# MLP up product by halves of the tokens, with all seven split weights of a block held

## The chip, the cores and the metric

The kernel runs on one core of one Trainium2 chip. The metric is the time of one execution on the device in microseconds (us). Before the change the median of 3 runs is 2862.23 us, the lowest 2861.79 and the highest 2864.47.

## The reference

One inference step of a trunk with two layers (DEPTH = 2), D_MODEL = 1024, D_FF = 4096. The prompt (16 meta tokens and 1024 frames) and 32 sample frames share the weights. Layer 0 mixes by a windowed attention and a gated linear attention, layer 1 by a forgetting attention; after each mixer comes the MLP, and only the MLP and the norm in front of it are touched here:

```python
def mlp(h, w_up, w_down):
    u = jax.nn.relu(h @ w_up)
    return (u * u) @ w_down
...
        xp = xp + mlp(rmsnorm(xp, norm_mlp[l]), w_up[l], w_down[l])
        xs = xs + mlp(rmsnorm(xs, norm_mlp[l]), w_up[l], w_down[l])
```

## The kernel before, in words

All arithmetic is fp32. TensorE multiplies in a reduced form (fp32r), so each operand is split into a high and a low part (hi_lo, L62): ScalarE casts the high part (L64), VectorE subtracts it from the source to give the low part (L66), or GpSimd does that where the caller passes "g" (L68). Each product of two operands is then three matmuls, hi by hi, hi by lo and lo by hi (mm3, L72 to L77).

The activations of a layer stay in SBUF as xT, features on the partitions, tokens on the columns. The tokens are four quarters q0 to q3 of 268 columns in layer 0 and 264 in layer 1 (qw); a half c has one column range of two quarters. The MLP's up product is done with seven products in place of eight for each 2x2 of blocks (list UP): the weights A11, A12, A22 and the sums S1 to S4 are multiplied by the activations B11, B21, B22 and the differences T1 to T4. A block is 128 columns of each half of w_up; there are 16 blocks, seven products in each, and each product has two token halves c = 0, 1 of 4 x 3 = 12 matmuls. That makes 16 x 7 x 2 x 12 = 2688 matmuls a layer. In the tables below a "group" is such a set of 12.

- **Operands.** After the mixer's output projection adds a quarter into xT (L833), mlp_norm squares it on ScalarE (L134), adds the squares on VectorE and GpSimd (L136), takes the mean on TensorE (L145), and scales the quarter on VectorE (L873, eight instructions). For q0 and q1 the result is split into B11 and B21; for q2 and q3 mlp_sums makes T1 (L884), T2 (L886), T3 (L888) and T4 (L890) on VectorE and splits each and B22. One such instruction has 128 x 1072 elements. All these subtractions and the low parts are VectorE's.
- **Weights.** up_load (L903) brings the raw block by a DMA from SyncE's queue, up_weights makes S1 to S4 (L914, L917, L920, L923) and splits each weight into a tile mu_w of five buffers, four products ahead of TensorE.
- **Order.** The loop in up takes a block product by product, and in each product both token halves. In mlp, TensorE's instructions stand in the order of the code (tc.manual_schedule); those of the other engines and of SyncE's queue are ordered by a scheduler that runs over the whole program. mlp makes T and B22 of q2 (first half), then squares q3 with two products of block 0 put between squares and scale, then makes T and B22 of q3 (second half).
- **Results.** Copies and adds from PSUM (ScalarE L974, L978, L980, L983; VectorE L976, L981, L985), squares (L989, L996) and the four differences that the down product needs (L1000) lie in columns of xT that are no longer needed; a DMA on SyncE's queue (L1001) writes them to ud in HBM, block by block. A separate tile, mu_early, takes part of block 0.
- **Down product.** down loads the weights k1 with four DMAs of 1 MB (L1018), splits all sixteen weight rows into md_w0 to md_w15, loads the activations ud as md_ur (L1058, three ahead), splits them into md_u, and runs 14 passes of 16 x 12 matmuls. Small GpSimd copies (behind, L1064) hold the loads of k2 back until a given md_u is there.

## Time and profile before

| | |
|---|---|
| median of 3 runs | 2862.23 us |
| profiled execution, its time | 2855.66 us |
| its span, mean granted TensorE clock | 2853.9 us, 0.963 |
| busy: PE, DVE, ACT, POOL | 92%, 66%, 44%, 20% |
| up product, layer 0 and layer 1 | about 619 to 973 us, 2137 to 2486 us |
| DMA traffic | 393.77 MB, 138 GB/s on average |

The profile is one execution, seen by the hardware profiler; its times count from the start of the span. PE is TensorE, DVE VectorE, ACT ScalarE, POOL GpSimd, SP SyncE (SPq its DMA queue). A row of the timeline gives the start, the busy time of a run of like instructions, the engine, the line, out<-in with the tiles' names, and their number; in brackets stands how long the engine had been idle and what ended that. Matmuls overlap by a little, so the start-to-start step of two rows is the better measure of one. A row of the table by stretches gives the busy time and the number of instructions (x) of PE, its weight loads (PEld), DVE, ACT and POOL, then the granted clock, the busy share of the DMA engines and GB/s.

### The profile page before, as it was taken

Reading aid. Unit: us, or ns where it says so; the run is one execution under the profiler, and the core shown is the slowest. Engines: PE = TensorE matmul, PEld = TensorE weight load, DVE = VectorE, ACT = ScalarE, POOL = GpSimd, SP = SyncE. Lnnn points to the kernel's source line nnn. Section 1 sums busy time; section 2 is a strip of 40 time slices with the busy share of each in tenths; the row PEclk is TensorE's granted clock in tenths of the full one; section 3 lists DMA queues with packets and bytes.
Section 4 is the critical chain, followed back from the end, with each engine's and each line's share of the span. In section 5 each row is a group of like instructions: output and inputs, shape, how many; then the busy total and the mean of one; then the engine's idle time right before and its main releaser. Section 6 shows DMA issues by size and latency. Waiting matters only on the chain.

```text
span 2853.9 us, 49119 instructions
## 1 busy us (share of the span) xinstructions
...
## 2 busy tenths in 40 slices
...
GB/s 192 100 134 104 72 140 45 30 120 101 151 129 164 202 231 218 168 134 121 123 193 168 115 176 127 89 101 102 77 91 79 144 147 144 164 274 205 200 138 105
DMA packets 371286, 393.77 MB, mean 138 GB/s; under 512 B 41503, under 2 KB 300280, under 8 KB 369000
## 3 DMA queue, kind: packets, MB, share of 16 engines
...
q8 instruction: 145, 2.38, 0.4%
q14 instruction: 93, 0.76, 0.1%
HBM read 263.94 MB, written 125.48 MB: 136 GB/s over the span
## 4 chain that ended last, share of the span: by engine, by line
PE 63%; issue 16%; DVE 9%; DMA 3%; ACT 2%; SPq 1%; POOL 1%; DVEq 0%; ACTq 0%; POOLq 0%
PE bank L75 11%; PE bank L76 11%; PE bank L77 11%; PE mu_y L77 5%; PE mu_y L76 5%; PE mu_y L75 5%; PE bank L1470 2%; PE bank L1480 1%; PE bank L1481 1%; PE fx_s L1452 1%; PE fx_s L1453 1%; DMA md_raw<-in_w_down 1%; PE bank L257 1%; DVE gl_Q L600 1%; PE b L701 1%
## 5 line engine op out<-in xcount | busy, mean ns | idle before, releaser
L75 PE MATMUL bank<-pj_wh,h 128*128 128x384 f32 (+3 forms) x832 | 298.0, 360 | 9.4 <-ACT pj_wh L64 7.0
L77 PE MATMUL bank<-pj_wh,h 128*128 128x384 f32 (+3 forms) x832 | 295.9, 357 | 6.0 <-DVE h L66 4.8
L76 PE MATMUL bank<-pj_wl,h 128*128 128x384 f32 (+3 forms) x832 | 297.3, 358 | 3.5 <-DVE pj_wl L66 3.5
L75 PE MATMUL mu_y<-md_u,md_w 128*128 128x268 f32 (+1 forms) x896 | 259.4, 289 | 26.9 <-ACT md_u L64 26.9
L76 PE MATMUL mu_y<-md_u,md_w 128*128 128x268 f32 (+1 forms) x896 | 257.8, 288 | 2.4 <-DVE md_u L66 2.4
L77 PE MATMUL mu_y<-md_u,md_w 128*128 128x268 f32 (+1 forms) x896 | 257.3, 287 | 0.0
L75 PE MATMUL bank<-md_u,md_w 128*128 128x268 f32 (+1 forms) x896 | 257.1, 287 | 0.0
L77 PE MATMUL bank<-md_u,md_w 128*128 128x268 f32 (+1 forms) x896 | 255.2, 285 | 0.0
L76 PE MATMUL bank<-md_u,md_w 128*128 128x268 f32 (+1 forms) x896 | 254.9, 285 | 0.0
L64 ACT CAST md_u<-md_ur 128x536 fp32r<-128x536 f32 (+1 forms) x224 | 141.1, 635 | 210.7 <-PE mu_y L77 110.7
L66 DVE TENSOR_TENSOR md_u<-md_ur,md_u 128x536 fp32r<-128x536 f32 (+1 forms) x224 | 157.9, 710 | 114.2 <-ACT md_u L64 113.8
L76 PE MATMUL mu_y<-ho_T,mu_w 128*128 128x268 f32 (+1 forms) x768 | 219.8, 286 | 0.2 <-DVE ho_T L66 0.2
L77 PE MATMUL mu_y<-ho_T,mu_w 128*128 128x268 f32 (+1 forms) x768 | 219.9, 286 | 0.0
L75 PE MATMUL mu_y<-ho_T,mu_w 128*128 128x268 f32 (+1 forms) x768 | 219.2, 285 | 0.0
L75 PEld LDWEIGHTS mu_y<-md_u,md_w 128*128 128x128 f32 x896 | 171.1, 191 | 27.4 <-ACT md_u L64 27.3
L66 DVE TENSOR_TENSOR mu_w<-mu_raw,mu_w 128x512 fp32r<-128x512 f32 x160 | 110.0, 688 | 117.0 <-ACT mu_w L64 117.0
L1283 POOL TENSOR_TENSOR fx_p<-fx_p,sm_den 128x144 f32<-128x144 f32 (+7 forms) x128 | 150.6, 1177 | 181.8 <-DVE sm_den L1282 164.7
L64 ACT CAST mu_w<-mu_raw 128x512 fp32r<-128x512 f32 x160 | 99.2, 622 | 188.6 <-PE bank L77 124.6
L75 PEld LDWEIGHTS bank<-pj_wh,h 128*128 128x128 f32 x832 | 158.8, 191 | 22.3 <-ACT pj_wh L64 7.5
L76 PEld LDWEIGHTS mu_y<-md_u,md_w 128*128 128x128 f32 x896 | 170.9, 191 | 3.5 <-DVE md_u L66 3.4
L77 PEld LDWEIGHTS bank<-pj_wh,h 128*128 128x128 f32 x832 | 158.6, 191 | 17.5 <-DVE h L66 5.1
L76 PEld LDWEIGHTS bank<-pj_wl,h 128*128 128x128 f32 x832 | 159.0, 191 | 16.3 <-DVE pj_wl L66 5.2
...
## 6 DMA issues: line engine op xcount, KB each, us to landing
...
ud<-xT SPq DMA_DIRECT2D x16, 1876.0 KB
...
```

Of the source, the lines that this page charges most:

```text
L64: nc.scalar.copy(hi, src)
L66: nc.vector.tensor_tensor(lo, src, hi.bitcast(F32), op=ALU.subtract)
L75: mm(out, ah, bh, start=start, stop=False)
L76: mm(out, ah, bl, start=False, stop=False)
L77: mm(out, al, bh, start=False, stop=stop)
L257: nc.tensor.matmul(*args, start=k == x == 0, stop=k == KB - 1 and x == 1)
L600: eng.tensor_tensor(ov, xv[r, :, :, 1], qv[r, :, :, 1], op=ALU.mult)
L701: nc.tensor.matmul(po[:m, h % 2, h // 2], att[:, h, :m], v[:, P * h:P * h + P], start=True, stop=False)
L1283: nc.gpsimd.tensor_tensor(p[:, :n], p[:, :n], den[:, 0:1].to_broadcast([P, n]), op=ALU.mult)
L1452: nc.tensor.matmul(s[:, a:b], qa[:, qc], ka[:, t0 + a:t0 + b], start=True, stop=False)
L1453: nc.tensor.matmul(s[:, a:b], qb[:, qc], kb[:, t0 + a:t0 + b], start=False, stop=ma >= mb)
L1470: nc.tensor.transpose(pt[:m, P * j:P * j + P], pr[j][:, k0:k0 + m], self.ident)
```

## The change

- **Order of the up product.** The unit is now one block and one token half. Block 0's first half goes first: A11, A12, S2, S1, S3. From then on the remaining products of a unit alternate with the first of the next one, by the list `late`. Every weight is used for half 0 and five or more groups later for half 1, so all seven split weights of a block are held, each in its own tile of one buffer; the next block's version is made after the half-1 use.
- **Who makes the low parts.** Block 0's seven weights, T4 and B22 have their low parts made on POOL (the "g" of hi_lo). The square of B21 goes from DVE to ACT.
- **Start in mlp.** The squares of q3 stand first, then block 0's load and its seven weights, then mlp_sums(2), four product steps, the scale of q3 (now mlp_scale, L883) and mlp_sums(3). The operands of each token half have tiles of their own.
- **Places of the results.** Even blocks put theirs in the columns of q0 and q1, odd ones in those of q2 and q3. The write to ud is issued by POOL instead of SP.
- **Down product.** The first k1 load and three activation loads stand ahead of the other three k1 loads; only six weight rows are written ahead of the passes, the other ten inside the first pass.
- **Norm buffers.** The squares use three buffers of nm_t in place of four, and the small part that fed from lx_t or nm_f uses nm_t.

The core of the diff:

```diff
@@ -130,7 +130,7 @@
...
-            sq = acc[e] if first else sb.tile([P, QMAX], F32, name="nm_t", bufs=4)[:, :w]
+            sq = acc[e] if first else sb.tile([P, QMAX], F32, name="nm_t", bufs=3)[:, :w]
...
@@ -211,18 +211,18 @@
...
         if few:
-            t0 = (sb.tile([P, D], F32, name="lx_t", bufs=3) if n == 0 else sb.tile([P, 384], F32, name="nm_f"))[:, :KB * few]
...
+            for k0 in range(0, KB, 4):
+                t0 = sb.tile([P, w], F32, name="nm_t", bufs=bufs)[:, :4 * few].rearrange("p (k f) -> p k f", f=few)
...
@@ -849,15 +849,17 @@
...
+    def operand(self, x, src, q, lo_eng="v"):
+        t = self.ho[x, q % 2]
+        self.hi_lo(src, t[:, 0], t[:, 1], lo_eng)
...
@@ -865,15 +867,20 @@
...
     def mlp_norm(self, q, between=()):
-        nc = self.nc
-        y = self.norm(self.qs[q], between)
+        finish = self.squares(self.qs[q])
+        for step in between:
+            step()
+        self.mlp_scale(q, finish())
...
+    def mlp_scale(self, q, y):
         c0, c1 = self.qs[q]
         x = self.xT[:, :, c0:c1]
         for k in range(KB):
...
+            self.nc.vector.scalar_tensor_tensor(x[:, k], x[:, k], self.gain[:, 2 * self.l + 1, k:k + 1], y, op0=ALU.mult, op1=ALU.mult)
...
@@ -885,121 +892,130 @@
...
-        sub(b21, b21, b11)
-        self.operand("T4", b21, q)
-        self.operand("B22", b22, q)
...
+        self.operand("T4", b21, q, "g")
+        self.operand("B22", b22, q, "g")
...
-    def up_load(self, b, sb):
...
+    def up_load(self, b, pool):
+        raw = pool.tile([P, KB, 2, P], F32, name=f"mu_raw{b % 2}", bufs=1)
...
+    def up_weights(self, x, w, pools, lo_eng):
...
             src = {"A11": a11, "A12": a12, "A22": a22}[x]
-        hl = sb.tile([P, 2, 4, P], F32R, name="mu_w", bufs=5)
-        self.hi_lo(src, hl[:, 0], hl[:, 1])
+        hl = pools[x not in ("A11", "A12")].tile([P, 2, 4, P], F32R, name=f"mu_w{x}", bufs=1)
...
-        early = sb.tile([P, hw], F32, name="mu_early", bufs=1)
+        units = [(b, c) for b in range(self.NP) for c in range(2)]
+        order = [(0, "A11"), (0, "A12"), (0, "S2"), (0, "S1"), (0, "S3")]
+        for u in range(len(units)):
+            late = [(u + 1, "A11"), (u, "A22"), (u + 1, "A12"), (u, "S4"), (u + 1, "S2"), (u + 1, "S1"), (u + 1, "S3")]
+            order += [x for x in late if x[0] < len(units)]
...
+        def weights(b, x):
+            ws[b, x] = self.up_weights(x, raws[b], pools, "v" if b else "g")
+
+        load(0)
+        for x in ("A11", "A12", "S1", "S2", "S3", "A22", "S4"):
+            weights(0, x)
+        yield
+        load(1)
+        for u, wn in order:
+            b, c = units[u]
+            w = ws[b, wn]
...
+            act = self.ho[self.UP[wn], c]
...
+            if wn == "A11":
+                if c == 0 and b:
+                    load(b + 1)
...
+            for k in range(4):
+                self.mm3(out, (w[:, 0, k], w[:, 1, k]), (act[:, 0, k], act[:, 1, k]), first and k == 0, k == 3, wn in ("S2", "S3", "A22", "S4"))
+            t = {x: y[:, cc] for x, y in v.items()}
+            if wn == "A11":
+                nc.scalar.copy(t["B11"], out)
...
+                nc.scalar.copy(t["B12"], out)
+            elif wn == "S3":
+                nc.scalar.copy(t["B22"], out)
+                tt(t["B22"], t["B22"], pr["z", u], op=ALU.add)
...
-                nc.sync.dma_start(self.ud[b // 4][:, b % 4], place[:, b % 2, 1:8, :hw])
...
+                        tt(v[x], v[p], v[m], op=ALU.subtract)
+                    nc.gpsimd.dma_start(self.ud[b // 4][:, b % 4], place[:, 1:8])
+
...
+                    for x in {"S2": (), "S1": ("S1", "S2")}.get(wn, (wn,)):
+                        weights(b + 1, x)
             yield
 
...
@@ -1063,8 +1079,6 @@
...
-        for x in range(4):
-            load(k1[x], "A11", 4 * x, 4)
...
@@ -1074,7 +1088,11 @@
...
-        for kb in range(NP):
+        load(k1[0], "A11", 0, 4)
+        ready(0)
+        for x in range(1, 4):
+            load(k1[x], "A11", 4 * x, 4)
+        for kb in range(6):
             w[0, kb] = weights(0, kb)
         at = 0
         out = {}
...
@@ -1088,6 +1106,8 @@
...
+                if n == 0 and c == 0 and kb + 6 < NP:
+                    w[0, kb + 6] = weights(0, kb + 6)
...
@@ -1132,14 +1152,19 @@
         with ExitStack() as st, tc.manual_schedule(engines={mybir.EngineType.PE}):
             ps = st.enter_context(tc.tile_pool(name="mlp", bufs=4, space=PSUM, reuse_waits="tile"))
             self.nm = pool(nms, "nml")
-            self.operands("ho2", ("T1", "T2", "T3", "T4", "B22"), "left")
-            with tc.tile_pool(name="mu", bufs=1, reuse_waits="tile") as sb:
-                steps = self.up(sb, ps)
-                self.mlp_sums(2)
-                self.mlp_norm(3, [partial(next, steps) for _ in range(2)])
-                self.mlp_sums(3)
-                for _ in steps:
-                    pass
+            pools = [pool(self.ups, "mua")]
+            self.operands("ho2", ("T2", "T1", "T3", "T4", "B22"), "left")
+            pools.append(pool(self.ups, "mub"))
+            finish = self.squares(self.qs[3])
+            steps = self.up(pools, ps)
+            next(steps)
+            self.mlp_sums(2)
+            for _ in range(4):
+                next(steps)
+            self.mlp_scale(3, finish())
+            self.mlp_sums(3)
+            for _ in steps:
+                pass
             self.ups.close()
             ks = ExitStack()
             kp = pool(ks, "mk", "right")

```

Line numbers after the change are larger by some: L884, L888, L886 and L890 (T1, T3, T2, T4) are L891, L896, L893 and L895, L914/L917/L920/L923 (S1, S2, S3, S4) are L921/L924/L926/L929, L873 is L883, L985 is L998, L989 is L1002, L1000 is L1013, L1001 is L1014, L1018 is L1034, L1058 is L1074. The lines L989 and L994 of after are the adds behind A12 and S3.

First place, the start of the up product in layer 0, VectorE. Before, around the scale of q3 (L873), the rows are the last weights of block 0, the sums of block 1, and the norm:

```order
L976 TENSOR_TENSOR mu_early<-mu_early,bank 128x268
L66 TENSOR_TENSOR mu_w<-mu_raw,mu_w 128x512
L976 TENSOR_TENSOR mu_early<-mu_early,bank 128x268
L66 TENSOR_TENSOR ho_T_6497<-xT,ho_T_6497 128x4x268
L66 TENSOR_TENSOR mu_w<-mu_raw,mu_w 128x512
L914 TENSOR_TENSOR mu_s<-mu_raw 128x512
L151 SCALAR_TENSOR_TENSOR nm_a<-bank,nm_a 128x268
L917 TENSOR_TENSOR mu_s<-mu_s,mu_raw 128x512
L920 TENSOR_TENSOR mu_raw<-mu_raw 128x4x128
L152 SCALAR_TENSOR_TENSOR nm_y<-nm_a,nm_y 128x268
L873 SCALAR_TENSOR_TENSOR xT<-xT,gain,nm_y 128x268 x8
L884 TENSOR_TENSOR xT<-xT 128x4x268
```

Ahead of the scale stand low parts of block 0's weights, the first sums of block 1 and the adds behind A12 of both halves; none of these rows reads a product later than A12. After, the rows around the scale of q3 (now L883) are:

```order
L929 TENSOR_TENSOR mu_raw_6542<-mu_raw_6542,mu_s 128x4x128
L66 TENSOR_TENSOR ho_T_6502<-xT,ho_T_6502 128x1072
L921 TENSOR_TENSOR mu_s<-mu_raw_6585 128x512
L989 TENSOR_TENSOR xT<-xT,bank 128x268
L926 TENSOR_TENSOR mu_raw_6585<-mu_raw_6585 128x4x128
L151 SCALAR_TENSOR_TENSOR nm_a<-bank,nm_a 128x268
L994 TENSOR_TENSOR xT<-xT,bank 128x268
L152 SCALAR_TENSOR_TENSOR nm_y<-nm_a,nm_y 128x268
L883 SCALAR_TENSOR_TENSOR xT<-xT,gain,nm_y 128x268 x8
L66 TENSOR_TENSOR mu_wA_6701<-mu_raw_6585,mu_wA_6701 128x512
L891 TENSOR_TENSOR xT<-xT 128x4x268
L66 TENSOR_TENSOR mu_wA_6732<-mu_raw_6585,mu_wA_6732 128x512
```

No low part of block 0's weights is left here. The scale now stands behind L994, which reads the result of S3, the fifth group of TensorE's new order; the second half's T1 to T4 (L891 and so on) come behind it.

The same place on POOL. Before, POOL has only the adds of squares and then nothing until the down product:

```order
L136 TENSOR_TENSOR nm_acc_6168<-nm_acc_6168,nm_t 128x268 x2
L136 TENSOR_TENSOR nm_acc_6325<-nm_acc_6325,nm_t 128x268 x2
L136 TENSOR_TENSOR nm_acc_6517<-nm_acc_6517,nm_t 128x268 x2
L1064 COPY md_k_10201<-md_u 1x1
L1064 COPY xT<-md_u 1x1 x4
```

After, these rows stand there (mu_wA and mu_wS are the seven weights of block 0, ho_B and ho_T are B22 and T4, first 6505 and 6506 for half 0, then 6510 and 6511 for half 1):

```order
L68 TENSOR_TENSOR mu_wA_6564<-mu_raw_6542,mu_wA_6564 128x512
L136 TENSOR_TENSOR nm_acc_6516<-nm_acc_6516,nm_t 128x268
L68 TENSOR_TENSOR ho_B_6506<-xT,ho_B_6506 128x1072
L68 TENSOR_TENSOR mu_wS_6553<-mu_s,mu_wS_6553 128x512
L68 TENSOR_TENSOR mu_wS_6561<-mu_raw_6542,mu_wS_6561 128x512
L68 TENSOR_TENSOR mu_wS_6557<-mu_s,mu_wS_6557 128x512
L68 TENSOR_TENSOR ho_T_6505<-xT,ho_T_6505 128x1072
L68 TENSOR_TENSOR mu_wS_6568<-mu_raw_6542,mu_wS_6568 128x512
L68 TENSOR_TENSOR ho_B_6511<-xT,ho_B_6511 128x1072
L68 TENSOR_TENSOR ho_T_6510<-xT,ho_T_6510 128x1072
L1014 DMA ud_6538<-xT 128x7x536 x4
L1014 DMA ud_6539<-xT 128x7x536 x4
```

POOL has taken five weight low parts (two more stand earlier), four low parts of 128 x 1072, and the ud writes.

Second place, the passage from the up to the down product of layer 0. VectorE before, where the rows md_w are the low parts of the down weights (the first twelve of the sixteen are left out) and md_u those of the activations:

```order
L66 TENSOR_TENSOR md_w_10248<-md_k_10200,md_w_10248 128x512
L66 TENSOR_TENSOR md_w_10251<-md_k_10200,md_w_10251 128x512
L66 TENSOR_TENSOR md_w_10254<-md_k_10200,md_w_10254 128x512
L66 TENSOR_TENSOR md_w_10257<-md_k_10200,md_w_10257 128x512
L66 TENSOR_TENSOR md_u<-md_ur,md_u 128x536 x3
L1032 TENSOR_TENSOR md_k_10201<-md_k_10201,md_raw 128x512 x3
```

and after:

```order
L1013 TENSOR_TENSOR xT<-xT 128x536 x4
L66 TENSOR_TENSOR md_w_10240<-md_k_10210,md_w_10240 128x512
L66 TENSOR_TENSOR md_w_10243<-md_k_10210,md_w_10243 128x512
L66 TENSOR_TENSOR md_w_10246<-md_k_10210,md_w_10246 128x512
L66 TENSOR_TENSOR md_w_10249<-md_k_10210,md_w_10249 128x512
L66 TENSOR_TENSOR md_u<-md_ur,md_u 128x536 x3
L66 TENSOR_TENSOR md_w_10252<-md_k_10211,md_w_10252 128x512
L66 TENSOR_TENSOR md_w_10255<-md_k_10211,md_w_10255 128x512
```

The three md_u rows that stood behind sixteen md_w rows stand behind four. The same place on SP's queue, before:

```order
L903 DMA mu_raw<-in_w_up 128x8x128 x2
L1001 DMA ud_6543<-xT 128x3752 x2
L1018 DMA md_k_10197<-in_w_down 128x4x512
L1018 DMA md_k_10198<-in_w_down 128x4x512
L1018 DMA md_k_10199<-in_w_down 128x4x512
L1018 DMA md_k_10200<-in_w_down 128x4x512
L1058 DMA md_ur<-ud_6540 128x2x268 x2
L1058 DMA md_ur<-ud_6541 128x2x268
L1018 DMA md_raw<-in_w_down 128x512 x2
L1001 DMA ud_6543<-xT 128x3752
L1018 DMA md_raw<-in_w_down 128x512
L1018 DMA md_k_10201<-in_w_down 128x4x512
```

and after:

```order
L910 DMA mu_raw_9288<-in_w_up 128x8x128 x2
L910 DMA mu_raw_9514<-in_w_up 128x8x128 x2
L910 DMA mu_raw_9740<-in_w_up 128x8x128 x2
L1034 DMA md_k_10210<-in_w_down 128x4x512
L1074 DMA md_ur<-ud_6538 128x2x268 x2
L1074 DMA md_ur<-ud_6539 128x2x268
L1034 DMA md_k_10211<-in_w_down 128x4x512
L1034 DMA md_k_10212<-in_w_down 128x4x512
L1034 DMA md_k_10213<-in_w_down 128x4x512
L1034 DMA md_raw<-in_w_down 128x512 x3
L1034 DMA md_k_10214<-in_w_down 128x4x512
L1074 DMA md_ur<-ud_6539 128x2x268
```

The ud writes have left the queue, so the loads of the down product stand directly behind the raw weights of the last block.

129 lines of the change are left out of this document (52 added, 77 removed).

## The prediction

> **What bounds the kernel now.** I read the page first: PE is busy for 92% of the span, so a change pays where PE is not busy. Then I cut the stretches around the two MLPs into windows; the columns are explained in the section on the profile.
>
> ```profile
> 600.00:620.00 20.00, 14.23 (x110) 13.60 (x108) 17.66 (x35) 9.66 (x19) 2.91 (x3) 1.00 0.39 116
> 620.00:640.00 20.00, 10.04 (x61) 9.62 (x60) 19.96 (x33) 8.02 (x14) 0.00 (x0) 0.76 0.52 144
> 640.00:660.00 20.00, 14.14 (x92) 13.61 (x93) 17.20 (x22) 9.58 (x15) 0.00 (x0) 0.73 0.04 10
> 680.00:960.00 280.00, 280.00 (x2273) 280.00 (x2272) 195.58 (x340) 94.64 (x202) 0.00 (x0) 1.00 0.44 138
> 960.00:980.00 20.00, 12.96 (x106) 12.74 (x104) 9.63 (x17) 6.43 (x14) 0.00 (x0) 0.87 0.59 221
> 980.00:1000.00 20.00, 12.92 (x82) 12.41 (x83) 13.44 (x23) 8.16 (x15) 2.75 (x7) 0.70 1.06 386
> 2140.00:2160.00 20.00, 9.88 (x60) 9.61 (x60) 19.96 (x33) 7.79 (x13) 0.00 (x0) 0.76 0.20 53
> 2180.00:2480.00 300.00, 300.00 (x2474) 300.00 (x2473) 205.94 (x362) 101.56 (x219) 0.00 (x0) 1.00 0.46 141
> ```
>
> In the middle of the up product PE is full: 2273 matmuls in 280 us, 0.1232 us each, 1.48 us per group of 12, at a clock of 1.00. VectorE (DVE) has 195.58 of 280 there, so it has room. At the start (620 to 640) it is the reverse: DVE 19.96 of 20, PE 61 matmuls where 162 fit, POOL nothing. At the passage to the down product (960 to 1000) both wait. Layer 1 repeats this. The waits of PE, from its timeline, are these:
>
> ```profile
> 619.58 0.39 PE L75 MATMUL mu_y<-ho_B,mu_w 128*128 128x268 f32 x1 [4.35 <-ACT mu_w L64]
> 622.21 0.59 PE L77 MATMUL mu_y<-ho_B,mu_w 128*128 128x268 f32 x1 [2.08 <-DVE mu_w L66]
> 643.73 0.59 PE L75 MATMUL bank<-ho_T,mu_w 128*128 128x268 f32 x1 [11.61 <-ACT ho_T L64]
> 646.23 0.59 PE L76 MATMUL bank<-ho_T,mu_w 128*128 128x268 f32 x1 [1.91 <-DVE ho_T L66]
> 986.29 0.59 PE L75 MATMUL mu_y<-md_u,md_w 128*128 128x268 f32 x1 [13.34 <-ACT md_u L64]
> 987.36 0.59 PE L76 MATMUL mu_y<-md_u,md_w 128*128 128x268 f32 x1 [0.47 <-DVE md_u L66]
> 2161.32 0.59 PE L75 MATMUL bank<-ho_T,mu_w 128*128 128x264 f32 x1 [10.52 <-ACT ho_T L64]
> 2499.10 0.59 PE L75 MATMUL mu_y<-md_u,md_w 128*128 128x264 f32 x1 [13.56 <-ACT md_u L64]
> ```
>
> So per layer there is a start of about 20 us of waiting, behind DVE's chain that makes the operands, and a passage of 13.8 us (13.34 + 0.47), behind DVE's low parts. The change acts on both.
>
> **The middle of the up product: no change.** The same 2688 matmuls run at PE's rate. DVE gains a little less work (the B21 square goes to ACT), ACT has 94.64 of 280. Each weight is now remade in a single buffer: between its half-1 use and its next use lie six other groups, 8.9 us. The tightest is S2, which needs S1 made first; it is worked out as a rival. I count zero.
>
> **The passage: a gain of about 7.5 us per layer.**
>
> ```profile
> 973.00 0.43 DVE L985 TENSOR_TENSOR xT<-xT,bank 128x268 f32<-128x268 f32 x1 [1.04 <-PE bank L77]
> 974.22 2.72 DVE L1000 TENSOR_TENSOR xT<-xT 128x536 f32<-128x536 f32 x4
> 976.85 9.82 DVE L66 TENSOR_TENSOR md_w<-md_k,md_w 128x512 fp32r<-128x512 f32 x16
> 986.59 1.96 DVE L66 TENSOR_TENSOR md_u<-md_ur,md_u 128x536 fp32r<-128x536 f32 x3
> ```
>
> Call 972.9, where the last group ends, E. DVE then finishes the results at 976.85 (E+3.9), makes sixteen low parts (9.82, 0.61 each) and only then the first md_u, so PE runs on from 987.36, E+14.5. After, the list has four low parts ahead of md_u: 3.9 + 4 x 0.61 + 0.65 = E+7.0, a gain of 7.5. The other twelve stand next on DVE at 0.61 each, faster than PE's 1.48 per weight row, so they stay ahead. PE still pauses for more than 3 us, so its slow clock after the pause (0.70 in the window) stays; it cancels. The k1 loads no longer queue behind ud writes; they land before E, which takes away ACT's waits there.
>
> What is late next: md_ur of the fourth group of activations. On SP it stands behind a k2 load that waits for a POOL copy, which itself stands behind POOL's last ud writes. Before, the load was issued at 987.85 and its DVE part ran at 998.12, 10.3 us later, with the queues at 1.06 and 386 GB/s:
>
> ```profile
> 987.85 0.53 SPq L1058 DMA_DIRECT2D md_ur<-ud  x1
> 998.12 0.71 DVE L66 TENSOR_TENSOR md_u<-md_ur,md_u 128x536 fp32r<-128x536 f32 x1
> ```
>
> After, it could issue at about E+8 and be ready at E+18; PE needs it six groups after E+7, with the slow clock for the first five us, at about E+18. So this may give back 0 to 3 us. I take 7.5, with 4 to 9 as bounds.
>
> **The start: a loss of about 6 us per layer.** Prices (start-to-start steps are 1.19 for 1072 elements, 0.60 for 512):
>
> ```profile
> 611.82 2.53 DVE L873 SCALAR_TENSOR_TENSOR xT<-xT,gain,nm_y 128x268 f32<-128x268 f32 x6
> 614.95 1.27 DVE L884 TENSOR_TENSOR xT<-xT 128x1072 f32<-128x1072 f32 x1
> 616.14 0.77 DVE L833 TENSOR_TENSOR xT<-xT,bank 128x268 f32<-128x268 f32 x2
> 621.47 0.68 DVE L66 TENSOR_TENSOR mu_w<-mu_raw,mu_w 128x512 fp32r<-128x512 f32 x1
> 622.07 0.68 DVE L914 TENSOR_TENSOR mu_s<-mu_raw 128x512 f32<-128x512 f32 x1
> 638.01 3.36 DVE L873 SCALAR_TENSOR_TENSOR xT<-xT,gain,nm_y 128x268 f32<-128x268 f32 x8
> ```
>
> Let t0 be 614.35, the end of q2's scale. Before, PE is free to go on with the second half's operand at 646.23, t0+31.9, with 61 up matmuls done. After, by PE's list, it stops before S2 of half 1, with nine groups, 108 matmuls, done. Those 47 more are worth 47 x 0.1232 = 5.8 us. When is the T2 of half 1 ready? DVE's list from t0 to T2 of half 0 has seven rows of 1072 elements, four of 512 and eight of 268 (0.35 each, by the 0.77 for two that overlap): 8.3 + 2.4 + 2.8 = t0+13.5. PE then runs S2 and S1, cold for five us (5.5), the mean (0.7) and S3 (1.5), t0+21.2; the add behind S3 and the end of the norm stand behind it, then the scale (3.4) to t0+26; then six rows of 1072, two of 512 and one add, 8.7, and 1.2 for T2's low part: t0+36. By this, 36 - 31.9 - 5.8 = -1.7, a small gain: the earlier products and the DVE work handed to POOL pay for a scale that now waits for S3.
>
> But POOL's part is not free. These rows show POOL and DVE at the same time:
>
> ```profile
> 1315.74 0.78 DVE L66 TENSOR_TENSOR h<-nm_t,h 128x268 fp32r<-128x268 f32 x2
> 1319.32 1.92 DVE L66 TENSOR_TENSOR h<-nm_t,h 128x268 fp32r<-128x268 f32 x2
> 1319.11 1.84 POOL L68 TENSOR_TENSOR h<-nm_t,h 128x268 fp32r<-128x268 f32 x2 [1.23 <-ACT h L64]
> 2120.52 3.06 POOL L136 TENSOR_TENSOR nm_acc<-nm_acc,nm_t 128x264 f32<-128x264 f32 x1 [4.69 <-ACT nm_t L134]
> 2120.57 2.41 DVE L66 TENSOR_TENSOR ho_B<-xT,ho_B 128x1056 fp32r<-128x1056 f32 x2
> 616.60 0.75 POOL L136 TENSOR_TENSOR nm_acc<-nm_acc,nm_t 128x268 f32<-128x268 f32 x1 [5.41 <-DVE xT L833]
> 1744.73 2.36 POOL L68 TENSOR_TENSOR fx_ml<-fx_ot,fx_mh 128x1024 fp32r<-128x1024 f32 x1 [1.62 <-ACT fx_mh L64]
> 1745.17 0.69 DVE L66 TENSOR_TENSOR fk_l<-bank,fk_h 128x512 fp32r<-128x512 f32 x1 [1.01 <-ACT fk_h L64]
> ```
>
> Two DVE low parts take 0.78 where they are not held up, but 1.92 behind POOL's two, and the four as a whole 2.13 (1319.11 to 1321.24), about the 1.5 (two at the 0.75 of 616.60, as wide) and 0.78 added up. At 2120.52 a POOL add of 0.75 takes 3.06: it ends half a microsecond after DVE's 2.41. So with both inputs in SBUF they take turns. Where DVE reads PSUM ("bank"), as at 1745.17 beside the POOL row of 1744.73, its 0.69 is that of 621.47.
>
> The Trainium skill ("SBUF — State Buffer", the section on the two separate sides) states this as a rule: a DVE operation with two SBUF inputs and a GpSimd operation that reads SBUF hold a shared port pair exclusively, and the loser blocks for the whole instruction. The trace agrees, 2.13 elapsed against 2.28 added; by the rule alone the start would cost the upper end below.
>
> POOL's rows at the start are five low parts of 512 at 1.25 (half of the 2.36 for 1024 elements, and some fixed time), two of 1072 at 2.45 and two adds at 0.75: 12.7 us, of which DVE's PSUM reads and waits cover some. I placed the rows of both lists one by one, each taking its turn when its operands are there and the other has ended, DVE first on a tie: T2 of half 0 is then at t0+19 and its weight at t0+21.5, and S2 of half 1 starts at t0+46. That gives 46 - 31.9 - 5.8 = +8.3; with POOL first, t0+48.4, +10.7. Between -1.7 and +10.7 the rows lie near +8.3; I take +6, since DVE's wait for S3 and its adds from PSUM may leave POOL more room than my turns do. The first wait of PE at t0 (4.35 + 2.08) goes in any case, since A11 now stands among the last projection groups, and is in the counts above.
>
> **Small terms.** Block 0's raw weights, 1 MB, now stand ahead of one load of the mixer's output weights on SP. At 386 GB/s that is 2.7 us if nothing covers it, else 0; I take 1 in layer 0, 0 in layer 1. The ud writes move to POOL:
>
> ```profile
> zb<-sw_z POOLq DMA_DIRECT2D x32, 194.0 KB, 2.3
> ud<-xT SPq DMA_DIRECT2D x16, 1876.0 KB
> ```
>
> POOL's own DMAs land 2.3 us after the issue for 194 KB. For 1876 KB that is 5 us at 386 GB/s, or 22 us scaled by size. The place is written again a block later, with some 12 us of slack, so I take 0. The Trainium skill ("DMA: Bandwidth & Descriptors", the anatomy of a GpSimd DMA) gives 2 us plus the bytes over 436 GB/s, an estimate of 6.4 us; by that the term is 0 as well, and no run here shows a large write on this queue.
>
> The norm buffers also shift the order of the first stage, where PE is idle for half of the first 50 us:
>
> ```profile
> 0.00:50.00 50.00, 23.56 (x119) 20.95 (x120) 20.43 (x56) 22.19 (x45) 10.80 (x13) 1.00 0.65 207
> ```
>
> Transposes of later chunks come earlier in the list, some projections later. The total work is the same; I take 0, within 5 either way.
>
> **Sum.** 2 x (+6 - 7.5) + 1 = -2 us on the profiled 2855.66. The median of the runs is 2862.23, 6.6 above it; the change is carried over to the median: 2860 us.
>
> **Rivals.**
> - *They don't take turns enough to matter.* The start gives -1.7 per layer: 2 x (-1.7 - 7.5) + 1 = -17, 2845 us. For it: 1744.73 and the DVE waits for PE, in which POOL is free. Against: 1319.11 and 2120.52.
> - *POOL goes first and the list is worse than worked out.* +10.7 per layer and 3 given back at the passage: 2 x (10.7 - 4.5) + 1 = +13, 2875 us. It decides where DVE finds POOL's two 1072 rows ahead of T1 and T2.
> - *The middle stalls, slower.* After the half-1 S1 group, DVE must make S1's low part, the S2 sum and S2's low part, behind the add of S3 and a square: 1.5 for S3, 0.8 for copy and add, then 0.6, 0.6, 0.7, 0.6, about 5 us, against five groups, 7.4 us. From 2.5 us more on (one run of four L1000 rows, 2.72, in between is enough) each block stalls. At 0.7 us in 30 blocks: +21, 2881 us. The same comes of ud writes that take over 12 us. Against: DVE idles for 30% of the middle.
> - *Not what it says:* the scheduler's list could have left DVE's chain as it was. The list shows otherwise, so this gets no share of its own.
>
> **Chances.** Forecast 0.48, turns without cost 0.25, POOL first 0.13, middle stalls 0.10, rest (first stage) 0.04. One measurement can tell about 0.2%, 5.7 us: faster than 2856.5, slower than 2868. The forecast's own range, 2853 to 2868, puts 0.11 of its 0.48 below 2856.5 and 0.02 above 2868. Faster: 0.25 + 0.11 = 0.36; slower: 0.13 + 0.10 + 0.02 + 0.02 = 0.27; same 0.37. For 8 in 10 the range takes in the first two rivals, 2842 to 2877, and leaves out the stalls and half of the edges.
>
> **What would show it.** Right: S2 of half 1 starts 40 to 46 us after the end of q2's scale, with POOL's L68 rows of 1072 elements over 3 us beside DVE's; PE's wait at the passage is about 6.5 in place of 13.34; windows in the middle stay 20.00 of 20. Wrong: PE waits inside the middle, a start before t0+38, or a passage above 10 us.

## The result, and the profile after

The changed kernel takes 2897.55 us (median of 4 runs, 2894.24 to 2900.16) against 2863.35 us before (4 runs, 2861.79 to 2867.05): a ratio of 1.0117, 95% interval 1.0099 to 1.0134. It is slower by 34 us, where 2860 us and a range up to 2877 us were forecast. The profiled execution took 2900.16 us, with a span of 2898.4 us and a mean TensorE clock of 0.950 (before 2855.66, 2853.9 and 0.963), so the two traces lie 44.5 us apart.

Cut at the same landmarks of PE, this is where the 44.5 us are (us; "up" runs from the last matmul of the output projection to the last one of the up product, "passage" from there to the first matmul of the down product's second pass, `bank<-md_u`; in layer 1 the projection's end is marked by its last matmul on the tile `fk_h`, some 4 us ahead of its very last one, before and after alike):

| stretch | before | after | difference |
|---|---|---|---|
| start to the second half of layer 0's output projection | 557.7 | 555.6 | -2.1 |
| second half of that projection | 57.2 | 63.9 | +6.7 |
| up, layer 0 | 357.8 | 368.8 | +11.0 |
| passage, layer 0 | 41.0 | 47.0 | +6.0 |
| down product to the first score product of layer 1 | 629.7 | 631.7 | +2.0 |
| layer 1 from there to the second half of its projection | 446.7 | 454.4 | +7.7 |
| second half of that projection | 36.7 | 37.0 | +0.3 |
| up, layer 1 | 358.4 | 370.8 | +12.3 |
| passage, layer 1 | 41.3 | 41.8 | +0.5 |
| down product to the end | 327.3 | 327.4 | +0.1 |

The places that the change touches (projections, up, passages) hold 36.8 us, about the 34 us of the medians. The 7.7 us in the middle can be chance for the greater part: that stretch took 446.7 to 451.3 us in four profiled kernels whose MLP start is that of before, and 447.9 to 457.3 us in the ten others of this study. A mean difference of some 3 us between the two groups is left unexplained.

The windows of the changed kernel, for the stretches shown of before (same columns):

```profile
620.00:640.00 20.00, 1.29 (x11) 1.08 (x9) 20.00 (x17) 8.16 (x13) 13.29 (x7) 0.59 0.16 55
660.00:680.00 20.00, 13.50 (x91) 13.51 (x92) 15.41 (x19) 8.40 (x14) 2.49 (x1) 0.71 0.00 1
680.00:960.00 280.00, 280.00 (x2268) 280.00 (x2268) 189.76 (x324) 101.09 (x215) 13.85 (x14) 1.00 0.43 144
980.00:1000.00 20.00, 11.02 (x75) 10.29 (x74) 10.01 (x17) 5.61 (x11) 2.91 (x6) 0.81 0.59 199
1000.00:1020.00 20.00, 11.25 (x72) 10.74 (x71) 13.02 (x22) 8.47 (x15) 1.50 (x2) 0.76 1.06 387
```

The middle of the up product is as full as before. The window 620 to 640 is the one to look at: DVE reads 20.00 of 20 busy, but with 17 rows where it had 33, and POOL is busy for 13.29 where it had nothing. Busy time counts the time in which an instruction is held up. The rows differ in size, so their number alone is no measure; but at the start-to-start steps of rows that nothing held up (1.19 us for 1072 elements, 0.60 for 512, 0.35 for 268) the 17 rows are an estimated 11.4 us of work, where the 33 of before were the full 20. Some 8.6 us DVE stood still. PE had 61 matmuls there and now has 11. From 660 to 680 PE is short once more, where before it was busy for 20.00 of 20. At the passage it is short over two windows, from 980 to 1020.

PE's waits in the changed kernel, from its timeline, first the two starts, then the two passages:

```profile
641.54 0.59 PE L75 MATMUL mu_y<-ho_T,mu_wS 128*128 128x268 f32 x1 [20.25 <-ACT xT L987]
666.50 0.59 PE L75 MATMUL mu_y<-ho_T,mu_wS 128*128 128x268 f32 x1 [11.13 <-ACT xT L987]
996.59 0.59 PE L75 MATMUL mu_y<-md_u,md_w 128*128 128x268 f32 x1 [8.05 <-ACT md_u L64]
997.64 0.59 PE L76 MATMUL mu_y<-md_u,md_w 128*128 128x268 f32 x1 [0.46 <-DVE md_u L66]
1015.88 0.59 PE L75 MATMUL mu_y<-md_u,md_w 128*128 128x268 f32 x1 [6.97 <-ACT md_u L64]
1018.25 0.59 PE L76 MATMUL mu_y<-md_u,md_w 128*128 128x268 f32 x1 [1.78 <-DVE md_u L66]
2188.92 0.59 PE L75 MATMUL mu_y<-ho_T,mu_wS 128*128 128x264 f32 x1 [25.02 <-ACT xT L987]
2213.07 0.59 PE L75 MATMUL mu_y<-ho_T,mu_wS 128*128 128x264 f32 x1 [11.00 <-ACT xT L987]
2532.74 0.59 PE L75 MATMUL mu_y<-md_u,md_w 128*128 128x264 f32 x1 [3.28 <-ACT md_u L64]
2536.54 0.59 PE L76 MATMUL mu_y<-md_u,md_w 128*128 128x264 f32 x1 [3.22 <-DVE md_u L66]
2551.92 0.39 PE L75 MATMUL mu_y<-md_u,md_w 128*128 128x264 f32 x1 [4.04 <-ACT md_u L64]
2554.35 0.59 PE L76 MATMUL mu_y<-md_u,md_w 128*128 128x264 f32 x1 [2.04 <-DVE md_u L66]
```

At each start PE waits twice, 20 to 25 us for S2 of half 0 and 11 us for S2 of half 1, where before it waited for 11.61 us once, after two short waits of 4.35 and 2.08. The releaser named is ACT's copy of A11's result out of PSUM (L987), and that copy itself waited for DVE:

```profile
641.11 0.38 ACT L987 COPY xT<-mu_y 128x268 f32<-128x268 f32 x1 [0.57 <-DVE ho_T L66]
```

It started as DVE's low part of T2 ended (639.81 + 1.26, below), and that low part is S2's operand as well. So DVE's chain sets the start. At each passage there is now a second pause, 8.75 us in layer 0 (6.97 + 1.78) and 6.08 in layer 1, that before did not have.

**The start.** DVE from t0, the end of q2's scale (615.18 + 3.74 = 618.92), and POOL beside it:

```profile
615.18 3.74 DVE L883 SCALAR_TENSOR_TENSOR xT<-xT,gain,nm_y 128x268 f32<-128x268 f32 x8
...
623.32 3.51 DVE L896 TENSOR_TENSOR xT<-xT 128x1072 f32<-128x1072 f32 x1
...
636.96 2.93 DVE L929 TENSOR_TENSOR mu_raw<-mu_raw,mu_s 128x512 f32<-128x512 f32 x1
639.81 1.26 DVE L66 TENSOR_TENSOR ho_T<-xT,ho_T 128x1072 fp32r<-128x1072 f32 x1
...
649.43 0.44 DVE L151 SCALAR_TENSOR_TENSOR nm_a<-bank,nm_a 128x268 f32<-128x268 f32 x1 [5.74 <-ACT nm_a L150]
...
650.71 3.36 DVE L883 SCALAR_TENSOR_TENSOR xT<-xT,gain,nm_y 128x268 f32<-128x268 f32 x8
```

```profile
623.07 2.63 POOL L68 TENSOR_TENSOR ho_B<-xT,ho_B 128x1072 fp32r<-128x1072 f32 x1
...
636.81 2.53 POOL L68 TENSOR_TENSOR ho_T<-xT,ho_T 128x1072 fp32r<-128x1072 f32 x1
```

The DVE row at 623.32 is one subtraction of 1072 elements, 1.27 for the same form before. It starts 0.25 us behind POOL's low part and ends at 626.83, 1.13 us after that one's end at 625.70: it stood still for as long as POOL ran. At 636.96 a DVE row of 512 elements (0.68) takes 2.93 in the same way. Then DVE, on whose chain PE waits, is idle for 5.74 us ahead of L151: the mean that it waits for stands on PE behind S2 and S1 of half 0, and S2 itself started at 641.54. So the scale of q3 ends at 654.07, t0+35.2. S2 of half 1 starts at 666.50, t0+47.6; in layer 1 at t0+47.8.

**The passage.** What SP waited for between 900 and 1010, and its issues there; then what it had issued before the change:

```profile
SPq L1034 <- PE bank L77: 57.7, 1, 57.7
```

```profile
988.61 0.37 SPq L1034 DMA_DIRECT2D md_k<-in_w_down  x1
989.15 1.57 SPq L1074 DMA_DIRECT2D md_ur<-ud  x3
990.77 2.28 SPq L1034 DMA_DIRECT2D md_k<-in_w_down  x3
...
1003.41 2.26 SPq L1074 DMA_DIRECT2D md_ur<-ud  x1
...
2524.40 0.37 SPq L1034 DMA_DIRECT2D md_k<-in_w_down  x1
...
2528.04 2.38 SPq L1034 DMA_DIRECT2D md_k<-in_w_down  x3
...
2536.51 2.60 SPq L1074 DMA_DIRECT2D md_ur<-ud  x1
```

```profile
970.03 3.88 SPq L1018 DMA_DIRECT2D md_k<-in_w_down  x4
```

In layer 0 the first k1 load (L1034) sat at the head of SP's queue for 57.7 us, until the last matmul of the up product (L77, the group of B22 and S4 of half 1) had ended, though nothing in the data ties the two. So the tile `md_k10` must lie in memory that held the operand B22 of half 1, and the load into it waited for the last reader of that; the run e2_k1_place below tests this. Everything behind it on the queue waited along: in layer 0 no load of the down product was issued before E (988.26 + 0.28 = 988.5; E is the end of the last up matmul), and the fourth load of activations went out only at 1003.41, E+14.9. In layer 1 (E at 2529.45) the first k1 load went out 5.1 us ahead of E, as the group of S1 and T1 of half 1 ended, the other three from 1.4 us ahead of E on. Before the change all four k1 loads went out at 970.03, 2.9 us ahead of E.

### The profile page after: what moved, and what is told of

Read it like the earlier page. It is cut to its first block, busy times and chain, and to the rows that moved or that the text cites. A ratio compares the mean times of both kernels' runs of the same rounds, so it can differ in the third digit from the quotient of the medians.

```text
span 2898.4 us, 49101 instructions
## 1 busy us (share of the span) xinstructions
PE 2650.0 (91%) x18391; PEld 2461.7 (85%) x18391; DVE 1885.9 (65%) x3804; ACT 1281.9 (44%) x2854; POOL 638.5 (22%) x665
## 4 chain that ended last, share of the span: by engine, by line
PE 65%; DVE 6%; DMA 3%; issue 3%; ACT 1%; SPq 0%; POOL 0%; DVEq 0%; ACTq 0%; POOLq 0%
PE bank L75 10%; PE bank L77 10%; PE bank L76 10%; PE mu_y L75 8%; PE mu_y L76 7%; PE mu_y L77 7%; PE bank L1495 3%; PE bank L1505 2%; PE bank L1506 1%; PE fx_s L1477 1%; PE fx_s L1478 1%; DMA md_raw<-in_w_down 1%; DMA md_k<-in_w_down 1%; PE bank L257 1%; DVE xT L883 1%
## 5 line engine op out<-in xcount | busy, mean ns | idle before, releaser
L75 PE MATMUL bank<-pj_wh,h 128*128 128x384 f32 (+3 forms) x832 | 297.5, 360 | 12.3 <-ACT h L64 4.2
L77 PE MATMUL bank<-pj_wh,h 128*128 128x384 f32 (+3 forms) x832 | 296.5, 357 | 0.1
L75 PE MATMUL mu_y<-md_u,md_w 128*128 128x268 f32 (+1 forms) x896 | 262.6, 293 | 22.3 <-ACT md_u L64 22.3
L76 PE MATMUL mu_y<-md_u,md_w 128*128 128x268 f32 (+1 forms) x896 | 261.2, 292 | 7.5 <-DVE md_u L66 7.5
L77 PE MATMUL mu_y<-md_u,md_w 128*128 128x268 f32 (+1 forms) x896 | 260.3, 290 | 0.0
L77 PE MATMUL bank<-md_u,md_w 128*128 128x268 f32 (+1 forms) x896 | 255.7, 285 | 0.0
L75 PE MATMUL mu_y<-ho_T,mu_wS 128*128 128x268 f32 (+1 forms) x512 | 149.2, 291 | 67.4 <-ACT xT L987 67.4
L75 PEld LDWEIGHTS mu_y<-md_u,md_w 128*128 128x128 f32 x896 | 174.1, 194 | 23.2 <-ACT md_u L64 23.2
L76 PEld LDWEIGHTS mu_y<-md_u,md_w 128*128 128x128 f32 x896 | 174.0, 194 | 8.9 <-DVE md_u L66 8.9
L77 PEld LDWEIGHTS mu_y<-md_u,md_w 128*128 128x128 f32 x896 | 173.7, 194 | 0.0
L75 PEld LDWEIGHTS bank<-md_u,md_w 128*128 128x128 f32 x896 | 168.9, 189 | 0.1
L76 PEld LDWEIGHTS bank<-md_u,md_w 128*128 128x128 f32 x896 | 168.9, 188 | 0.1
L77 PEld LDWEIGHTS bank<-md_u,md_w 128*128 128x128 f32 x896 | 168.8, 188 | 0.0
L77 PEld LDWEIGHTS bank<-pj_wh,h 128*128 128x128 f32 x832 | 159.0, 191 | 10.9 <-POOL h L68 0.4
```

The lines of the kernel that those rows point to most:

```text
L75: mm(out, ah, bh, start=start, stop=False)
L76: mm(out, ah, bl, start=False, stop=False)
L77: mm(out, al, bh, start=False, stop=stop)
```

## The experiments

The account under test has three causes: (1) DVE and POOL take turns at the start, and the scale of q3 waits behind S2, both in full; (2) the k1 loads are held up by the memory they lie in, and crowd the load that is needed next; (3) block 0's raw weights delay the projection's weights. The expectations name the theories that they weigh in their own text. Landmarks for all runs that bear on it, as in the first table (us, one profiled execution each; ratio to before with its 95% interval from the timed runs):

| kernel | projection, layer 0 | up, layers 0 and 1 | passage, layers 0 and 1 | ratio |
|---|---|---|---|---|
| before | 57.2 | 357.8, 358.4 | 41.0, 41.3 | 1 |
| after | 63.9 | 368.8, 370.8 | 47.0, 41.8 | 1.0117 (1.0099 to 1.0134) |
| e2_k1_place | 62.8 | 366.6, 370.6 | 34.7, 34.2 | 1.0067 (1.0051 to 1.0084) |
| e3_lo_dve | 65.7 | 362.7, 361.8 | 47.0, 41.9 | 1.0072 (1.0054 to 1.0089) |
| e5_k1_lo | 63.7 | 362.0, 362.5 | 35.2, 34.1 | 0.9994 (0.9977 to 1.0011) |
| e6_raw_late | 61.1 | 368.0, 370.8 | 46.9, 41.8 | 1.0101 (1.0079 to 1.0123) |
| e7_scale_early | 62.6 | 363.0, 362.8 | 46.8, 42.0 | 1.0056 (1.0036 to 1.0075) |
| e8_all | 62.2 | 357.0, 357.9 | 34.5, 34.6 | 0.9950 (0.9932 to 0.9968) |
| e12_s1_first | 60.9 | 357.7, 357.7 | 34.5, 34.6 | 0.9967 (0.9955 to 0.9979) |

Half an interval is about 0.17%, 5 us. The landmarks within a stretch are the sharper tool: the six kernels that keep the place of k1 and the down product of after have passages of 46.7 to 47.0 us in layer 0, and a second profile of the kernel before gave passages of 42.7 and 43.3 us and an up product of 357.9 us in layer 0, so that these marks repeat to about 2 us at worst.

### The kernel before, once more

> The kernel before, unchanged, as a control for what one profile differs from another. Between the two profiles shown, 7.7 us more were spent in the attention of layer 1 (from its first score product to the end of its output projection), where the change edits nothing. If that is chance of one execution, this profile shows a stretch there that lies between the two, off by some us from the 446 us of the first. If it is the change (buffers, order), it is within 1 us of 446.

One run of the unchanged kernel: 2859.0 us, span 2857.2. The stretch of layer 1 that differed by 7.7 us between the two profiles took 451.3 us here, 4.6 more than in the first profile of the same kernel. So 4.6 of the 7.7 us need no cause in the change.

### The k1 tiles in other memory

```
-            k1, k2 = ([kp.tile(...) ...] for x in (1, 2))
+            k2, k1 = ([kp.tile(...) ...] for x in (2, 1))
```

> The kernel after, with one edit: k2's tiles are allocated ahead of k1's in their pool, so k1 lies where B11 and B21 lay and not where B22 of half 1 lay. Theory A (the place): in the changed kernel SP's first load of the down product waits for the last matmul of S4, since its tile lies on that product's operand; with other memory below it the loads are issued at least 8 us before the end of the up product, PE's first wait at the passage falls from 8.05 us to about 6, and the second wait in the first pass (8 us in layer 0, 6 in layer 1) is gone; 15 to 24 us less than the changed kernel, some 2875 us. Rival B (the queues): the passage is held by the transfers themselves, with the DMA engines full after the end of the up product whatever the order; then the time moves by less than 5 us.

Only the places of the tiles change: k2, which is needed later, takes the place that k1 had. The ratio falls to 1.0067, some 14 us. SP, then PE, then ACT's copy of the fourth activations, at the passage of layer 0 (E at 987.9):

```profile
967.93 0.37 SPq L1034 DMA_DIRECT2D md_k<-in_w_down  x1
...
975.34 4.93 SPq L1034 DMA_DIRECT2D md_k<-in_w_down  x3
...
995.01 0.59 SPq L1074 DMA_DIRECT2D md_ur<-ud  x1
```

```profile
995.04 0.59 PE L76 MATMUL mu_y<-md_u,md_w 128*128 128x268 f32 x1 [4.45 <-DVE md_u L66]
```

```profile
1004.19 0.64 ACT L64 CAST md_u<-md_ur 128x536 fp32r<-128x536 f32 x1 [6.71 <-DMA md_ur<-ud]
```

The loads go out 20 and 13 us ahead of E, PE goes on at 995.04, E+7.1, the fourth activations are there at 1004.19, and PE makes no second pause. Both passages are 34.7 and 34.2 us, 6.3 and 7.1 better than before and 12.3 and 7.6 better than after (the timed runs put the gain over after at 14 us, give or take 7): cause 2 is shown, and the forecast gain exists once the loads are early.

### All low parts back on DVE

```
-        self.operand("T4", b21, q, "g")
-        self.operand("B22", b22, q, "g")
+        self.operand("T4", b21, q)
+        self.operand("B22", b22, q)
...
-            ws[b, x] = self.up_weights(x, raws[b], pools, "v" if b else "g")
+            ws[b, x] = self.up_weights(x, raws[b], pools, "v")
```

> The kernel after, with the low parts of block 0's weights, of T4 and of B22 made on VectorE again; all else as after. Theory C (turns): POOL and DVE take turns at two-input work from SBUF, and POOL's rows are twice as long; with all of it on DVE the first S2 starts at about 17 us after the end of q2's scale in place of 22.6, and S2 of half 1 about 6.5 us sooner; 10 to 14 us less than the changed kernel over both layers. Rival D (POOL's help is real and the start is lost to the scale that waits for S3): 5.4 us more of DVE work per layer, so 6 to 11 us more.

The ratio falls to 1.0072, some 13 us, although DVE has four rows of 1072 and seven of 512 more to do at each start. DVE's two subtractions and PE's two waits at the start of layer 0:

```profile
623.44 1.26 DVE L896 TENSOR_TENSOR xT<-xT 128x1072 f32<-128x1072 f32 x1
...
633.99 0.69 DVE L929 TENSOR_TENSOR mu_raw<-mu_raw,mu_s 128x512 f32<-128x512 f32 x1
```

```profile
636.34 0.59 PE L75 MATMUL mu_y<-ho_T,mu_wS 128*128 128x268 f32 x1 [14.56 <-ACT xT L987]
660.57 0.59 PE L75 MATMUL mu_y<-ho_T,mu_wS 128*128 128x268 f32 x1 [10.38 <-ACT xT L987]
```

3.51 becomes 1.26, 2.93 becomes 0.69, and with t0 at 619.40 S2 of half 1 starts at t0+41.2 instead of 47.6. Half of cause 1 is shown: work given to POOL here cost more than doing it on DVE.

### The down product's part alone, in the kernel before

```
-        for x in range(4):
-            load(k1[x], "A11", 4 * x, 4)
...
-        for kb in range(NP):
+        load(k1[0], "A11", 0, 4)
+        ready(0)
+        for x in range(1, 4):
+            load(k1[x], "A11", 4 * x, 4)
+        for kb in range(6):
             w[0, kb] = weights(0, kb)
...
+                if n == 0 and c == 0 and kb + 6 < NP:
+                    w[0, kb + 6] = weights(0, kb + 6)
```

> The kernel before, with the change's edit of the down product alone (first k1 load and three activation loads ahead, six weight rows ahead of the passes, ten inside). By theory A its k1 tile is free about 3 us before the end of the up product here, so the passage gains what was forecast, 4 to 7.5 us per layer: 8 to 15 us less than before, 2848 to 2855 us. By rival B (transfers) nothing is gained, or the fourth activation load stalls the first pass by as much: within 4 us of before.

No gain: 2861.83 us, ratio 1.0001 (0.9989 to 1.0013). The number that the theory gave for this kernel fell; what happened is the second half of rival B, that the fourth activation load stalls the first pass by as much. PE at the passage (E at 968.2), then the load of the fourth activations and ACT's copy of them, and ACT's copy of the fourth ones in layer 1 of after:

```profile
973.25 0.59 PE L75 MATMUL mu_y<-md_u,md_w 128*128 128x268 f32 x1 [5.05 <-ACT md_u L64]
975.27 0.59 PE L76 MATMUL mu_y<-md_u,md_w 128*128 128x268 f32 x1 [1.42 <-DVE md_u L66]
991.68 0.59 PE L75 MATMUL mu_y<-md_u,md_w 128*128 128x268 f32 x1 [5.01 <-ACT md_u L64]
994.01 0.59 PE L76 MATMUL mu_y<-md_u,md_w 128*128 128x268 f32 x1 [1.74 <-DVE md_u L66]
```

```profile
975.53 2.00 SPq L1058 DMA_DIRECT2D md_ur<-ud  x1
...
990.99 0.64 ACT L64 CAST md_u<-md_ur 128x536 fp32r<-128x536 f32 x1 [7.90 <-DMA md_ur<-ud]
```

```profile
2551.24 0.63 ACT L64 CAST md_u<-md_ur 128x528 fp32r<-128x528 f32 x1 [5.28 <-DMA md_ur<-ud]
```

The first pause falls from 13.8 to 6.47 us, as forecast, and a second one of 6.75 us takes it back: the same as in layer 1 of after. The fourth md_ur load was issued at 975.53 (E+7.3) and copied at 990.99, 15.5 us later; in layer 1 of after it was issued at E+7.1 and took 14.7 us; in e2 it was issued at E+7.1, no earlier, but was copied at 1004.19, after 9.2 us. What differs is when the four k1 loads, 1 MB each, were issued: the first 2.9 us before E in e4 and 5.1 in layer 1 of after, the other three from 0.5 and 1.4 us before E on; in e2 the first went out 20 us before E and the others from 13 us before E on, the last of them 9 us before. The queues move about 390 GB/s here (0.39 MB per us), so by estimate 4 MB are some 10 us of their time. So k1 loads issued near E delay not the first activations, which go right behind the first of them, but the fourth.

### Both repairs together

The edits of e2 and e3.

> The kernel after with both edits of before: k1's tiles where B11 and B21 lay, and all low parts on VectorE. The two took 16 and 17 us off the changed kernel apart; theory A and theory C act at different places (the passage, the start), so they add up: 33 us less than the changed kernel, 2862 to 2868 us. If they were one cause seen twice (fewer GpSimd instructions, a warmer clock), the sum is clearly less than 33, some 2873 us or more.

2861.22 us, ratio 0.9994: level with before. The two repairs add up (-0.50% and -0.45% from 1.0117 would give 1.0022; four intervals of some 0.17% each stand behind that number; by the landmarks of the projection, the ups and the passages they take 23 and 13 us off the changed kernel apart and 35 together), and the up product is still 4 us a layer longer than before, so that something of the start was left.

### Raw weights of block 0 later

```
+        if not b:
+            self.nc.gpsimd.tensor_copy(raw[0:1, 0, :, 0:1], self.ho["B11", 0][0:1, 0, 0:2, 0:1].bitcast(F32))
```

The small copy, ahead of the loads of the raw weights, makes them wait until B11 of half 0 is there, past the projection's weights.

> The kernel after, where block 0's raw load of w_up is held back until the operand B11 of q0 exists, by a copy of two elements on GpSimd into its tile. Theory E: the 1 MB ahead of the loads of the mixer's output weights makes these late; TensorE's two waits for op_h in layer 0 (3.43 and 3.27 us) shrink to the 2.0 in all of the kernel before, and the output projection of layer 0 takes 59 us in place of 63.9; 4 to 5 us less than the changed kernel. Rival F: the extra 5 us come of the A11 matmuls put among the projection's, which wait for POOL's low part; then the time stays within 2 us.

Waits of PE for the projection's weights between 550 and 620, in after and in this kernel (in all, how often, the longest):

```profile
PE bank L75 <- ACT op_h L64: 6.7, 2, 3.4
```

```profile
PE bank L75 <- ACT op_h L64: 4.6, 5, 3.3
```

One of the two long pauses is gone, the other is not. The projection falls from 63.9 to 61.1 us; over all kernels with the early load it took 62.6 to 65.8, in the three with the late one 60.9 to 62.2. The ratio, 1.0101, does not differ from 1.0117 by more than the intervals. So cause 3 shows in the landmark alone, with 2.8 us here and 2.6 between the means of the two groups; an estimated 1.5 of the rest are the twelve A11 matmuls that moved in (0.1232 us each), and some 2.4 stay open (before took 59.0 with the norm buffers alone, so part of that may be theirs or chance).

### The scale of q3 ahead of S2

```
-            for _ in range(4):
+            for _ in range(2):
                 next(steps)
             self.mlp_scale(3, finish())
```

> The kernel after, with the scale of q3 two product steps earlier, so that its mean stands ahead of S2 on TensorE and the scale no longer waits for S3's result on VectorE. Theory G: the scale's place (VectorE idle for 5.74 us ahead of L151 at 649.43, since the mean stands behind S2 and S1 on TensorE) sets the start of the second half; S2 of half 1 starts 6 to 8 us sooner, 10 to 16 us less than the changed kernel over two layers. Rival C alone (turns of POOL and DVE): the freed time goes into turns with POOL's rows, and less than 5 us is gained.

```profile
635.67 1.26 PE L145 MATMUL bank<-nm_acc,mean 128*128 128x268 f32 x2 [15.81 <-DVE nm_acc L139]
640.12 0.59 PE L75 MATMUL mu_y<-ho_T,mu_wS 128*128 128x268 f32 x1 [3.19 <-ACT xT L987]
659.63 0.59 PE L75 MATMUL mu_y<-ho_T,mu_wS 128*128 128x268 f32 x1 [6.14 <-ACT xT L987]
```

The mean (L145) now stands ahead of S2 on PE, and DVE scales before it would wait. S2 of half 1 starts at 659.63, with t0 at 617.50, t0+42.1 instead of 47.6. The ratio is 1.0056, and the up products are 5.8 and 8.0 us shorter. With POOL's work unchanged this is the other half of cause 1.

### All repairs

The edits of e2, e3, e6 and e7.

> The kernel after with all four edits: k1's place, low parts on VectorE, the raw load held back, the scale early. If the theories add up: 16 + 17 + 5 + 12 = 50 us less than the changed kernel, 2847 us, which is 0.5% below the kernel before. If the early scale only moves the wait (VectorE is full from the scale of q2 on in this version), some 2858 us.

2850.51 us, ratio 0.9950 (0.9932 to 0.9968): faster than both kernels. With t0 at 614.08, PE's S2 of both halves:

```profile
631.01 0.59 PE L75 MATMUL mu_y<-ho_T,mu_wS 128*128 128x268 f32 x1 [0.94 <-ACT xT L989]
650.53 0.59 PE L75 MATMUL mu_y<-ho_T,mu_wS 128*128 128x268 f32 x1 [6.12 <-ACT xT L989]
```

L989 is the line that was L987 in after. The two groups start at t0+16.9 and t0+36.5. The up product is 0.8 and 0.5 us shorter than before, each passage 6.5 and 6.7 shorter, the two projections 5.0 and 2.9 longer: -6.6 us in sum, where the timed runs give -14, with -9 as the nearer end of the interval. The rest isn't placed.

### The ud writes on SP again

```
-                    nc.gpsimd.dma_start(self.ud[b // 4][:, b % 4], place[:, 1:8])
+                    nc.sync.dma_start(self.ud[b // 4][:, b % 4], place[:, 1:8])
```

> The kernel after, with the 32 ud writes on SP's queue again, as before the change. If the software queue costs time (rival: ud writes that land late, 7.7 us against what SP's need, and POOL's 1.0 us of issue each), up to 10 us less than the changed kernel. If it costs nothing, as forecast, the time stays within 3 us: TensorE has no wait in the middle of the up product of the changed kernel (280.00 of 280 us), and the passage is held by k1's place, which stays as it is.

2892.87 us, ratio 1.0116 (1.0103 to 1.0129): the same as after. Writing by POOL's queue neither costs nor brings anything that these runs can tell. The page of after has these writes as

```profile
ud<-xT POOLq DMA_DIRECT2D x16, 1876.0 KB, 7.7
```

with 7.7 us from issue to landing, under the 12 us of slack.

### The norm buffers alone, in the kernel before

```
-            sq = ... sb.tile([P, QMAX], F32, name="nm_t", bufs=4)[:, :w]
+            sq = ... sb.tile([P, QMAX], F32, name="nm_t", bufs=3)[:, :w]
...
+        bufs = 4 if n == 0 else 3
...
+            for k0 in range(0, KB, 4):
+                t0 = sb.tile([P, w], F32, name="nm_t", bufs=bufs)[:, :4 * few].rearrange("p (k f) -> p k f", f=few)
...
+                self.hi_lo(t0, h[:, k0:k0 + 4, 0:few], h[:, k0:k0 + 4, 64:64 + few])
```

> The kernel before, with the change's norm buffers alone (three buffers of nm_t for squares, the small part in nm_t and not in lx_t or nm_f). Forecast: the order of the first stage shifts, with no more than 5 us either way; the changed kernel came to the first matmul of the second part of layer 0's output projection 1.6 us sooner than before, so 0 to 3 us less than before. If the buffers make the norms of layer 1 wait, 3 to 8 us more.

2861.75 us, ratio 0.9998 (0.9988 to 1.0008): nothing.

### Which of POOL's rows hurt

As e3, but only T4 and B22 go back to DVE; the weights of block 0 stay on POOL.

> The kernel after, with the low parts of T4 and B22 on VectorE and those of block 0's seven weights left on POOL. It parts theory C: if the turns are lost to POOL's long rows (2.5 to 3.2 us for 1072 elements, twice in each half), this wins most of the 17 us that all low parts on VectorE won: 10 to 13 us less than the changed kernel, with the rest in the weights. If the 512 rows of the weights do it (five of them between the scales of q2 and q3), it wins under 7 us.

2888.68 us, ratio 1.0089 (1.0074 to 1.0104), between after and e3. With t0 at 617.56:

```profile
662.44 0.59 PE L75 MATMUL mu_y<-ho_T,mu_wS 128*128 128x268 f32 x1 [10.38 <-ACT xT L987]
```

S2 of half 1 is at t0+44.9: 2.7 of the 6.4 us that e3 gains come of the four wide rows, 3.7 of the seven weight rows; in layer 1 it is 4.3 of 8.2. The timed runs put about 8 of 13 us on the wide rows, with intervals that don't separate the two shares. Neither kind is harmless.

### S1 ahead of S2, with all repairs

The edits of e8, and in the order of block 0 `(0, "S1"), (0, "S2")` for `(0, "S2"), (0, "S1")`.

> The four edits of e8_all, and S1 ahead of S2 in block 0's first five products, since T1 is ready some 8 us before T2 (low parts at 621.09 and 629.28 to 632 in e8_all): TensorE can run S1 while it waits, one group (1.5 us, 3 at the slow clock) leaves the chain between T2 and the adds, and there is a pause less on the way to S2 of half 1 only if these adds hold VectorE up. From that 0 to 4 us less than e8_all, 2847 to 2851 us.

2851.86 us, ratio 0.9967 (0.9955 to 0.9979): the same as e8. Which of the two products comes first makes no difference here.

## Why the prediction was wrong

Its terms, layer by layer:

- *The start, "I take +6"*: mis-sized. By the prediction's own measure S2 of half 1 came at t0+47.6 and 47.8, net +9.9 and +10.9, and the up stretches grew by 11.0 and 12.3. That is near the end of the range that was worked out with POOL first (t0+48.4). The lists placed by turns were close: S2 of half 0 came at t0+22.6 where they had its operands at t0+21.5, S2 of half 1 at t0+47.6 where they had t0+46. The step that failed is the reason for going below them, from +8.3 to +6: that "DVE's wait for S3 and its adds from PSUM may leave POOL more room". The turns were taken in full (3.51 and 2.93 for 1.27 and 0.68), and the wait of the scale, which stood in the lists, came as well: e3 takes away the one and gains 6.4 us at S2 of half 1, e7 the other and gains 5.5, e8 both and gains 11.1. The list without turns, t0+36, has no run of its own. In e3 DVE makes POOL's low parts itself, 5.4 us by its expectation, so that 41.4 would be due, and it came to t0+41.2; that e8, with the same rows and an early scale, came to t0+36.5 is a coincidence. The rule of the Trainium skill ("SBUF — State Buffer", the section on the two separate sides), that the loser of the shared port is held for the whole instruction, agrees with the rows at 623.07 and 623.32.
- *The passage, "a gain of about 7.5 us per layer"*: the chain behind it was right. PE went on at E+7.1 in layer 1 and in e2, where E+7.0 was forecast. Two other steps failed. "They land before E": in layer 0 the k1 loads were issued after E, and PE went on only at 997.64, E+9.1; in layer 1 three of the four were issued 1.4 us before E or later. I took the order of SP's list for the time of issue; what a list does not show is that a load must wait for the last reader of the memory that it goes into. And "this may give back 0 to 3 us": it gave back all and more. The point at which PE needs the fourth activations, about E+18, was right (it stood still from 2547.88 on, E+18.4), and so was the issue at about E+8 for layer 1 (E+7.1; in layer 0 it was E+14.9). The 10.3 us taken for the load, from a row of before where the k1 loads were long past, were 14.7 there, since the 4 MB of k1 were in the queues with it. On top, PE's second pause brings its slow clock a second time: the granted clock was 0.81 and 0.76 in the two windows from 980 to 1020, and after the pause that ended at 1018.25 matmuls came 0.22 us apart until 1023.1, then 0.12.
- *The raw load, "I take 1"*: 2.6 to 2.8 by e6, the top of its bounds of 0 to 2.7. The projection grew by 6.7, of which I had no more than this and the moved matmuls in view.
- *The middle, the ud writes and the norm buffers, 0 each*: right, by the window of 280.00, by e9 and by e10. For the writes the estimate from the Trainium skill ("DMA: Bandwidth & Descriptors", the anatomy of a GpSimd DMA) was 6.4 us; the trace has 7.7.

In the prediction's form the sum is 11.0 + 12.3 for the starts, 6.0 + 0.5 for the passages, and 6.7 + 0.3 for the projections, +36.8 in place of -2. The rival with POOL first had the start nearly right, but kept 4.5 us of gain at each passage; that every passage could lose all of its gain at the same time stood nowhere, and so the range ended at 2877. Of the signs named beforehand for being right, the full middle held; S2 of half 1 came at t0+47.6, just outside the 40 to 46; of POOL's four wide low parts in layer 0 one took over 3 us, and the longest rows were DVE's; and PE's first wait at the passage was 6.50 (3.28 and 3.22) in layer 1, as named, but 8.51 (8.05 and 0.46) in layer 0. Of the signs for being wrong, a passage above 10 us came true: PE's two pauses add up to 17.3 us in layer 0 and 12.6 in layer 1.
